# Seven-product units of a feed-forward layer: four weight sums in a row, and the offset tokens read from a copy in the first unit alone

## The chip, the core and the metric

One core of one Trainium2 chip runs the whole program. The metric is the device time of one execution in microseconds (us). TensorE (PE in the profile; its weight loads are PEld) multiplies, VectorE (DVE), ScalarE (ACT) and GpSimd (POOL) work on tiles in SBUF, and SyncE (SP) issues most transfers.

## The reference

A two-layer transformer over 256 latent and 256 context tokens, width 1024: in each layer a half feed-forward block, a mixer (attention, then mLSTM), and a second half feed-forward block. What the change touches is the first product of the feed-forward block:

```python
def half_ffn(h, shift, scale, gate, w_in, w_out, g, b):
    xm = modulate(h, shift, scale)
    a, u = jnp.split(xm @ w_in, 2, axis=-1)
    y = (jax.nn.silu(a) * u) @ w_out
    return post_norm(h, 0.5 * gate * y, g, b)
```

with D_FF = 2816, so `w_in` is 1024 x 5632, that is 22 blocks of 128 columns of `a` and as many of `u`.

## The kernel before

**Numbers.** Every fp32 operand of a product is held as a high part (fp32r) and a low part, the rest that the high part leaves out. `split` (L223 to L229) makes them: ACT casts to the high part (L224), DVE subtracts it to get the low part (L229). `mm3` (L238 to L245) does one product in three matmuls: high by high, high by low, low by high. All of them are recorded under L240. The split tokens are `xh` and `xl` (t3 and t4 in the order of instructions); 512 tokens are the columns, 256 latent (LAT) and 256 context (CTX).

**The units.** A feed-forward block runs over 22 units j, in two halves of 11 (`NFH`). A unit multiplies a column block of `w_in` with all tokens; after 11 units, `unit_out` multiplies the half's result with `w_out`. In the second half of two of the four blocks (second block of layer 0, first block of layer 1) the unit is `fast_in`: seven products of half size in place of eight (Strassen's scheme, in the form of Winograd). For this the tokens are combined once, ahead of the stage, in `fast_sums`, which runs beside the last `unit_out` products of the first half: it leaves one combination in the place of CTX tokens of `xh`/`xl` and puts three more, `made[0]`, `made[1]`, `made[2]`, into one tile (L582 to L587; t1185 in the first stage, t1681 in the second). The weights of a unit are combined anew in each unit: two raw chunks r0 and r1 (512 KB each) hold the blocks a11, a21, a12, a22, and four sums s1 to s4 are made of them by DVE (L625). Seven of these go through `split`: a11 alone, r1 (a12 and a22), s1 with s2, s4 with s3.

**The products of a unit,** in PE's order: a11, a12, s1, s2, a22, s4, s3. Each is 4 steps of 3 matmuls with 256 columns, 12 matmuls, so a unit has 84. Between them ACT copies results out of PSUM: L650 after a11 and L653 after s1 (both before the same PSUM tile is added to, by s2 and by s4), L655 after s2, L657 after a22. Then DVE adds (L659), ACT applies silu (L660), DVE forms the product (L663, L664), and the result is split for `unit_out`.

**Where the operands lie.** Split weights lie 16 elements (64 bytes) into their tile (`SH`). Six of the seven token operands begin on a multiple of 256 bytes. `made[2]`, the one of the product a22, begins `FLIP` = 56 elements (224 bytes) past one:

```python
x = self.t([P, 6 * n + FLIP], F32R, pool=st)
at = [2 * i * n + (FLIP if i == 2 else 0) for i in range(3)]
```

**Buffers and order.** Split weights live in a pool of 7 tiles (`WB`, tag "w"), which all stages share, raw chunks in a pool of 3 (`RAW`). The order of instructions on each engine is made by the framework's scheduler from the program's order and the pools; each engine runs its own row in order and waits at semaphores.

Of the kernel before, what the change touches and what calls it, by code (L numbers as in the profile page):

```python
# [9 lines left out]
F32 = mybir.dt.float32  # L10
F32R = mybir.dt.float32r
# [7 lines left out]
P = 128  # L19
# [3 lines left out]
TL = 256  # L23
# [4 lines left out]
NFH = 11  # L28
# [3 lines left out]
BLOCK = 64  # L32
# [11 lines left out]
WB = 7  # L44
# [45 lines left out]
FLIP = 56  # L90
# [81 lines left out]
class Body:  # L172
# [74 lines left out]
    def x(self, d, g):  # L247
        return self.xh[:, d, g[0] : g[1]], self.xl[:, d, g[0] : g[1]]
# [333 lines left out]
    def fast_operands(self, st):  # L582

        n = ND // 2 * TL
        x = self.t([P, 6 * n + FLIP], F32R, pool=st)
        at = [2 * i * n + (FLIP if i == 2 else 0) for i in range(3)]
        self.made = [[x[:, a + p * n : a + (p + 1) * n].rearrange("p (k f) -> p k f", f=TL) for p in range(2)] for a in at]  # L587

    def fast_sums(self, i):

# [25 lines left out]
    def fast_in(self, j, w_in, st):  # L616

        nc, V, S = self.nc, self.nc.vector, self.nc.scalar
        half = 4 * P
        r0, r1 = (self.raw(w_in[2 * j + i]) for i in range(2))  # L620
        sums = self.t([P, 4 * half], tag="sums", bufs=1, pool=st)
        part = lambda x, i: x[:, i * half : (i + 1) * half]
        a11, a21, a12, a22 = part(r0, 0), part(r0, 1), part(r1, 0), part(r1, 1)
        s1, s2, s4, s3 = (part(sums, i) for i in range(4))
        add = lambda o, x, y: V.tensor_tensor(out=o, in0=x, in1=y, op=ALU.add)  # L625
        ws = [self.pair(sh=SH, n=half)] + [self.pair(sh=SH) for _ in range(3)]
        self.split(a11, *ws[0])
        self.split(r1, *ws[1])
        add(s1, a21, a22)
        add(s2, s1, a11)  # L630
        self.split(sums[:, : 2 * half], *ws[2])
        add(s4, s2, a12)
        add(s3, a11, a21)
        self.split(sums[:, 2 * half :], *ws[3])
        w = {n: [part(x, i) for x in ws[p]] for n, p, i in (
            ("a11", 0, 0), ("a12", 1, 0), ("a22", 1, 1), ("s1", 2, 0), ("s2", 2, 1), ("s4", 3, 0), ("s3", 3, 1),
        )}
        of = lambda k0, g: lambda k: self.x(k0 + k, g)
        made = lambda i: lambda k: [x[:, k, :] for x in self.made[i]]

        def product(o, name, x, first, last):
            for k in range(ND // 2):
                c = slice(k * P, (k + 1) * P)
                self.mm3(o, [y[:, c] for y in w[name]], x(k), first and k == 0, last and k == ND // 2 - 1, group=False)

        x, yv, z = self.mm()[:, :TL], self.mm(), self.mm()[:, :TL]
        y, v = yv[:, :TL], yv[:, TL:]
        a, u = self.tmp(), self.tmp()
        product(x, "a11", of(0, LAT), True, False)
        S.copy(a[:, :TL], x)  # L650
        product(y, "a12", of(ND // 2, LAT), True, True)
        product(v, "s1", of(0, CTX), True, False)
        S.copy(u[:, TL:], v)  # L653
        product(x, "s2", made(0), False, False)
        S.copy(a[:, TL:], x)  # L655
        product(z, "a22", made(2), True, True)
        S.copy(u[:, :TL], z)  # L657
        product(v, "s4", of(ND // 2, CTX), False, True)
        V.tensor_tensor(out=a, in0=a, in1=yv, op=ALU.add)  # L659
        S.activation(a, a, AF.Silu)  # L660
        product(x, "s3", made(1), False, True)
        u2 = u.rearrange("p (n f) -> p n f", n=2)
        V.scalar_tensor_tensor(u2, x[:, None, :].broadcast_to([P, 2, TL]), -1.0, u2, ALU.mult, ALU.subtract)  # L663
        V.tensor_tensor(out=a, in0=a, in1=u, op=ALU.mult)  # L664
        gh, gl = self.gt[j] = tuple(self.t([P, self.gw], F32R, tag=k, bufs=self.gn, pool=self.gp) for k in ("gh", "gl"))
        self.split(a, gh, gl)
# [1071 lines left out]
```

## Time and profile before

| | us |
|---|---|
| median of 3 runs (lowest to highest) | 1640.27 (1639.47 to 1640.42) |
| the profiled execution, its whole time | 1640.61 |
| its span, first to last instruction | 1638.8 |
| first `fast_in` stage (11 units) | about 747 to 854 |
| second `fast_in` stage (11 units) | about 1102 to 1209 |

In the page, busy time is given for each engine with its share of the span; then groups of instructions by line, with their count, their busy time, the mean of one in ns, and the idle time of the engine just before them. In the timeline each row has the start, the time, the engine, the line and operation, tiles and sizes, a count, and in brackets the idle time before it with what ended it. A row of stretches has the stretch, its length, then for each engine the busy time and in brackets how many instructions ran, the granted PE clock as a share of full speed, and the share of the DMA engines with GB/s.

### The profile page before, as it was taken

What the parts mean: (1) busy time and instruction counts of PE and PEld (TensorE: products, weight loads), DVE (VectorE), ACT (ScalarE), POOL (GpSimd) and SP (SyncE); (2) the same over time, 40 slices, a digit from 0 to 9 for tenths busy, and PEclk for the clock granted to TensorE, in tenths of its full rate; (3) what the DMA queues carried; (4) which work ended last, traced back from release to release, by engine and by line L of the source; (5) the groups of instructions that cost most, each with busy time, mean ns of one, the idle gap of its engine ahead of it and who ended that gap; (6) DMA issues with size and microseconds to landing.
All of it is one profiled execution on the core that took longest, in us unless ns stands there. A gap on an engine that the chain in (4) does not pass through costs nothing. (4 is left out here: it accounts for less than half of the span.)

```text
span 1638.8 us, 26592 instructions
## 1 busy us (share of the span) xinstructions
PE 1616.8 (99%) x10308; PEld 1455.5 (89%) x10308; DVE 1353.5 (83%) x2689; ACT 745.4 (45%) x1269; POOL 62.0 (4%) x76
## 2 busy tenths in 40 slices
PE   9999999999999999999999999999999999999998
PEld 6888888889988998889998998889999989999987
DVE  5899977749889879899976979699966968897687
ACT  5622123214676443325652434335652657566542
POOL 0000000001011100000000100000001000020000
PEclk9999999999999999999999999999999999999999
DMA  9677766422202447633344258713363332437552
GB/s 362 221 232 245 238 198 193 140 78 85 65 2 78 150 134 220 218 115 117 116 145 177 78 161 289 252 63 110 103 220 102 97 129 91 139 102 251 181 176 92
DMA packets 72495, 252.59 MB, mean 154 GB/s; under 512 B 7984, under 2 KB 10800, under 8 KB 72368
## 3 DMA queue, kind: packets, MB, share of 16 engines
q1 hardware_dynamic: 71792, 250.10, 47.3%
q8 instruction: 81, 1.33, 0.3%
q10 hardware_dynamic: 576, 0.79, 0.1%
q14 instruction: 46, 0.38, 0.1%
HBM read 249.81 MB, written 1.05 MB: 153 GB/s over the span
## 5 line engine op out<-in xcount | busy, mean ns | idle before, releaser
L240 PE MATMUL t<-t,t 128*128 128x256 f32 (+2 forms) x8412 | 1323.0, 318 | 6.7 <-ACT t L224 3.1
L240 PEld LDWEIGHTS t<-t,t 128*128 128x128 f32 x8412 | 1191.7, 188 | 125.7 <-ACT t L224 4.6
L224 ACT CAST t<-t 128x1024 fp32r<-128x1024 f32 (+3 forms) x521 | 429.6, 844 | 493.8 <-PE t L240 232.8
L229 DVE TENSOR_TENSOR t<-t,t 128x256 fp32r<-128x256 f32 (+2 forms) x740 | 514.8, 729 | 119.1 <-ACT t L224 114.7
L340 DVE SCALAR_TENSOR_TENSOR t<-t,t 128x1024 bf16<-128x1024 f32 x224 | 260.7, 1219 | 0.0
L578 ACT ACTIVATE t<-t 128x512 f32<-128x512 f32 (+1 forms) x71 | 34.4, 489 | 107.4 <-PE t L240 107.4
L920 PE MATMUL t<-t,t 128*128 128x256 f32 (+1 forms) x256 | 79.3, 310 | 0.0
L922 PE MATMUL t<-t,t 128*128 128x256 f32 (+1 forms) x256 | 78.6, 307 | 0.0
L921 PE MATMUL t<-t,t 128*128 128x256 f32 (+1 forms) x256 | 78.3, 306 | 0.0
L702 DVE SCALAR_TENSOR_TENSOR t<-t,t,t 128x256 f32<-128x256 f32 x96 | 42.8, 478 | 41.4 <-PE t L240 41.2
L579 DVE TENSOR_TENSOR t<-t,t 128x512 f32<-128x512 f32 (+1 forms) x71 | 39.1, 553 | 44.5 <-PE t L240 30.8
L474 POOL TENSOR_TENSOR t<-t,t 128x256 f32<-128x256 f32 x30 | 23.3, 775 | 1117.2 <-ACT t L464 1115.7
L1435 PE MATMUL t<-t,t 128*128 128x512 f32 (+3 forms) x286 | 61.0, 368 | 1.7 <-ACT t L1512 1.0
L1435 PEld LDWEIGHTS t<-t,t 128*128 128x128 f32 (+2 forms) x286 | 43.8, 159 | 19.1 <-issue 3.7
L848 PE MATMUL t<-t,t 128*128 128x512 f32 (+1 forms) x300 | 60.5, 364 | 0.0
L848 PEld LDWEIGHTS t<-t,t 128*128 128x128 f32 x300 | 51.5, 189 | 9.0
L464 ACT ACTIVATE t<-t 128x256 f32<-128x256 f32 x72 | 26.1, 412 | 65.2 <-DVE t L457 65.2
L921 PEld LDWEIGHTS t<-t,t 128*128 128x128 f32 x256 | 48.1, 188 | 3.0 <-DVE t L229 0.5
L920 PEld LDWEIGHTS t<-t,t 128*128 128x128 f32 x256 | 48.2, 188 | 2.7
L922 PEld LDWEIGHTS t<-t,t 128*128 128x128 f32 x256 | 48.2, 188 | 2.6 <-DVE t L532 0.2
L625 DVE TENSOR_TENSOR t<-t,t 128x512 f32<-128x512 f32 x66 | 45.3, 687 | 1.2 <-DMA t<-in_ffn_in 0.6
L531 ACT ACTIVATE t<-t,t 128x256 fp32r<-128x256 f32 x72 | 32.8, 503 | 27.4 <-DVE t L530 27.4
(200 smaller groups left out, 1064.9 us busy)
## 6 DMA issues: line engine op xcount, KB each, us to landing
t<-in_ffn_in SPq DMA_DIRECT2D x168, 512.0 KB, 4.1
t<-in_ada_w SPq DMA_DIRECT2D x137, 512.0 KB, 4.3
t<-in_ffn_out SPq DMA_DIRECT2D x66, 512.0 KB, 4.4
t<-in_ffn_last SPq DMA_DIRECT2D x22, 512.0 KB, 3.6
t<-in_att_in SPq DMA_DIRECT2D x12, 512.0 KB, 3.5
t<-in_c SPq DMA_DIRECT2D x8, 512.0 KB, 7.1
t<-in_att_out SPq DMA_DIRECT2D x8, 512.0 KB, 3.5
t<-in_ml_qk SPq DMA_DIRECT2D x8, 512.0 KB, 3.8
```

Of the source, the lines that this page charges most:

```text
L224: self.behind(self.nc.scalar.copy(h, x))
L229: self.behind(self.nc.vector.tensor_tensor(out=ls, in0=xs, in1=hs.bitcast(F32), op=ALU.subtract))
L240: mm = lambda *k, **kw: self.nc.tensor.matmul(*k, skip_group_check=not group, **kw)
L340: ins = nc.vector.scalar_tensor_tensor(self.tmp().bitcast(BF16), r, 1.0, self.cb[:, v, :], ALU.mult, ALU.mult, accum_out=to)
L579: V.tensor_tensor(out=sl, in0=sl, in1=pu[:, :n], op=ALU.mult)
L625: add = lambda o, x, y: V.tensor_tensor(out=o, in0=x, in1=y, op=ALU.add)
L702: V.scalar_tensor_tensor(z, y[:, gg[0] - t0 : gg[1] - t0], gate()[:, v, d : d + 1], z, ALU.mult, ALU.add)
L848: pin(nc.tensor.matmul(o, gs[g], ws[k][w][:, i : i + n], start=k == k0 and g == w == 0, stop=k == k1 - 1 and g == 1,))
L920: mm(o, self.xh[:, k, c], wh, start=k == 0, stop=False)
L921: mm(o, self.xh[:, k, c], wl, start=False, stop=False)
L922: mm(o, self.xl[:, k, c], wh, start=False, stop=k == ND - 1)
L1435: mm = lambda *k, **kw: pin(nc.tensor.matmul(*k, **kw))
```

## The change

The sum and copy of the third token combination now stand like this. `made[2]` lies right behind the other two, on a multiple of 256 bytes; a spare tile of `FLIP` elements keeps the size of what the stage holds. In the first unit of each stage (j = 11) a tile of the weight pool is taken, ACT copies both halves of `made[2]` into it `FLIP` elements past its start, and the product a22 of this unit reads the copy; in the ten units behind it, a22 reads `made[2]` itself. In every unit the four sums are made in a row, and both splits of sums follow.

```diff
     def fast_operands(self, st):
         n = ND // 2 * TL
-        x = self.t([P, 6 * n + FLIP], F32R, pool=st)
-        at = [2 * i * n + (FLIP if i == 2 else 0) for i in range(3)]
-        self.made = [[x[:, a + p * n : a + (p + 1) * n].rearrange("p (k f) -> p k f", f=TL) for p in range(2)] for a in at]
+        x = self.t([P, 6 * n], F32R, pool=st)
+        self.t([P, FLIP], pool=st)
+        self.made = [[x[:, (2 * i + p) * n : (2 * i + p + 1) * n].rearrange("p (k f) -> p k f", f=TL) for p in range(2)] for i in range(3)]
...
     def fast_in(self, j, w_in, st):
         half = 4 * P
+        t4 = self.made[2]
+        if j == NFH:
+            w = self.t([P, 2 * 1024 + BLOCK], F32R, tag="w", bufs=WB)
+            t4 = [w[:, FLIP + i * 1024 : FLIP + (i + 1) * 1024].rearrange("p (k f) -> p k f", f=TL) for i in range(2)]
+            for i in range(2):
+                S.copy(t4[i], self.made[2][i].bitcast(F32))
...
         add(s1, a21, a22)
         add(s2, s1, a11)
-        self.split(sums[:, : 2 * half], *ws[2])
         add(s4, s2, a12)
         add(s3, a11, a21)
+        self.split(sums[:, : 2 * half], *ws[2])
         self.split(sums[:, 2 * half :], *ws[3])
...
-        product(z, "a22", made(2), True, True)
+        product(z, "a22", lambda k: [x[:, k, :] for x in t4], True, True)
```

The lines of the changed kernel are six further down from L620 on (L625 becomes L631, L650 becomes L656).

On PE, where the product a22 of the first unit of the first stage stands (t3 and t4 are `xh` and `xl`, t1185 holds the made sums; right of the arrow tokens, then weights), before:

```order
L240 MATMUL t1216_7168<-t4_68,t1213_7153 128x256
L240 MATMUL t1216_7168<-t3_67,t1213_7153 128x256
L240 MATMUL t1215_7167<-t1185_6936,t1213_7153 128x256 x12
L240 MATMUL t1217_7169<-t1185_6936,t1212_7152 128x256 x12
L240 MATMUL t1216_7168<-t3_67,t1214_7154 128x256
```

and now:

```order
L240 MATMUL t1218_7172<-t4_68,t1215_7157 128x256
L240 MATMUL t1218_7172<-t3_67,t1215_7157 128x256
L240 MATMUL t1217_7171<-t1185_6936,t1215_7157 128x256 x12
L240 MATMUL t1219_7173<-t1209_7147,t1214_7156 128x256 x12
L240 MATMUL t1218_7172<-t3_67,t1216_7158 128x256
```

The count and order of matmuls stay; the twelve of a22 read t1209, the copy, where they read t1185.

On ACT, from the splits of `fast_sums` to the first copy out of PSUM of the first unit, before (the casts of a11 and of r1, into t1211 and t1212, stand ahead of these rows, in front of those of `fast_sums`):

```order
L224 CAST t1185_6936<-t1199_7046 128x512
L224 CAST t1185_6936<-t1198_7044 128x512
L224 CAST t1185_6936<-t1201_7059 128x512
L224 CAST t1213_7153<-t1210_7150 128x1024
L224 CAST t1214_7154<-t1210_7150 128x1024
L224 CAST t1225_7273<-t1222_7268 128x512
L224 CAST t1226_7274<-t1223_7270 128x1024
L650 COPY t1218_7170<-t1215_7167 128x256
```

and now:

```order
L224 CAST t1185_6936<-t1200_7047 128x512
L224 CAST t1185_6936<-t1199_7045 128x512
L224 CAST t1185_6936<-t1202_7060 128x512
L625 CAST t1209_7147<-t1185_6936 128x1024
L224 CAST t1213_7155<-t1210_7150 128x512
L625 CAST t1209_7147<-t1185_6936 128x1024
L224 CAST t1214_7156<-t1211_7152 128x1024
L224 CAST t1215_7157<-t1212_7154 128x1024
L224 CAST t1216_7158<-t1212_7154 128x1024
L224 CAST t1227_7277<-t1224_7272 128x512
L224 CAST t1228_7278<-t1225_7274 128x1024
L656 COPY t1220_7174<-t1217_7171 128x256
```

The two copies (L625) are new, and the casts of a11 (t1213) and r1 (t1214) of the first unit now stand behind the last cast of `fast_sums`, one behind each copy.

On DVE, the work on the weights of the third unit of the first stage and on the output of its first unit, before:

```order
L625 TENSOR_TENSOR t1238_7394<-t1236_7390,t1237_7392 128x512
L229 TENSOR_TENSOR t1239_7395<-t1236_7390,t1239_7395 128x512
L625 TENSOR_TENSOR t1238_7394<-t1238_7394,t1236_7390 128x512
L625 TENSOR_TENSOR t1238_7394<-t1236_7390 128x512
L659 TENSOR_TENSOR t1218_7170<-t1218_7170,t1216_7168 128x512
L229 TENSOR_TENSOR t1240_7396<-t1237_7392,t1240_7396 128x1024
L663 SCALAR_TENSOR_TENSOR t1219_7171<-t1215_7167,t1219_7171 128x512
L229 TENSOR_TENSOR t1241_7397<-t1238_7394,t1241_7397 128x1024
L664 TENSOR_TENSOR t1218_7170<-t1218_7170,t1219_7171 128x512
L625 TENSOR_TENSOR t1238_7394<-t1238_7394,t1237_7392 128x512
L229 TENSOR_TENSOR t1221_7265<-t1218_7170,t1220_7264 128x512
L229 TENSOR_TENSOR t1242_7398<-t1238_7394,t1242_7398 128x1024
```

and now:

```order
L229 TENSOR_TENSOR t1241_7399<-t1238_7394,t1241_7399 128x512
L665 TENSOR_TENSOR t1220_7174<-t1220_7174,t1218_7172 128x512
L229 TENSOR_TENSOR t1242_7400<-t1239_7396,t1242_7400 128x1024
L669 SCALAR_TENSOR_TENSOR t1221_7175<-t1217_7171,t1221_7175 128x512
L631 TENSOR_TENSOR t1240_7398<-t1238_7394,t1239_7396 128x512
L670 TENSOR_TENSOR t1220_7174<-t1220_7174,t1221_7175 128x512
L631 TENSOR_TENSOR t1240_7398<-t1240_7398,t1238_7394 128x512
L631 TENSOR_TENSOR t1240_7398<-t1238_7394 128x512
L229 TENSOR_TENSOR t1223_7269<-t1220_7174,t1222_7268 128x512
L631 TENSOR_TENSOR t1240_7398<-t1240_7398,t1239_7396 128x512
L229 TENSOR_TENSOR t1243_7401<-t1240_7398,t1243_7401 128x1024
L229 TENSOR_TENSOR t1244_7402<-t1240_7398,t1244_7402 128x1024
```

The same twelve stand there in another order: the fourth sum (L631, from t1239) now comes ahead of the low part of the first pair (t1243), and the sums stand further back among the work of the unit before.

## The prediction, made before the changed kernel ran

> **What bounds the kernel now.** The page first. TensorE is busy for 99% of the span, nearly all of it in L240, and that line waited 6.7 us in all.
>
> ```profile
> span 1638.8 us, 26592 instructions
> ...
> PE 1616.8 (99%) x10308; PEld 1455.5 (89%) x10308; DVE 1353.5 (83%) x2689; ACT 745.4 (45%) x1269; POOL 62.0 (4%) x76
> ...
> L240 PE MATMUL t<-t,t 128*128 128x256 f32 (+2 forms) x8412 | 1323.0, 318 | 6.7 <-ACT t L224 3.1
> ```
>
> So time comes only from the spacing of matmuls or from a wait of PE. The stretches of two neighbouring units of the first seven-product stage, cut where their first products start, show no idle PE and the full granted clock (1.00), yet one is 9.7 us long and the other 9.8.
>
> ```profile
> 776.30:786.00 9.70, 9.70 (x87) 9.70 (x86) 9.61 (x14) 6.08 (x10) 0.00 (x0) 1.00 0.38 113
> 786.00:795.80 9.80, 9.80 (x87) 9.80 (x86) 8.98 (x13) 5.99 (x10) 0.00 (x0) 1.00 0.33 110
> ```
>
> Where inside a unit the difference arises is read from ACT's timeline: its copies out of PSUM wait for PE, so their starts mark the ends of products (L653 after s1, L655 after s2, L657 after a22). In the second stage:
>
> ```profile
> 1109.51 0.37 ACT L657 COPY t<-t 128x256 f32<-128x256 f32 x1 [0.52 <-PE t L240]
> ...
> 1116.33 0.37 ACT L653 COPY t<-t 128x256 f32<-128x256 f32 x1 [0.47 <-PE t L240]
> 1117.68 0.38 ACT L655 COPY t<-t 128x256 f32<-128x256 f32 x1 [0.99 <-PE t L240]
> ...
> 1119.09 0.37 ACT L657 COPY t<-t 128x256 f32<-128x256 f32 x1 [0.52 <-PE t L240]
> ...
> 1126.16 0.37 ACT L653 COPY t<-t 128x256 f32<-128x256 f32 x1 [0.67 <-PE t L240]
> 1127.57 0.37 ACT L655 COPY t<-t 128x256 f32<-128x256 f32 x1 [1.04 <-PE t L240]
> ...
> 1129.00 0.37 ACT L657 COPY t<-t 128x256 f32<-128x256 f32 x1 [0.54 <-PE t L240]
> ...
> 1138.58 0.37 ACT L657 COPY t<-t 128x256 f32<-128x256 f32 x1 [0.51 <-PE t L240]
> ```
>
> From the end of a22 to the end of the next unit's s1 lie five products (s4, s3, a11, a12, s1). They take 1116.33 - 1109.51 = 6.82 us the first time, 1.364 a product, and 1126.16 - 1119.09 = 7.07 the next, 1.414 a product. From a22 to a22 it is 9.58, 9.91, 9.58 us: PE has **two paces, and each a22 turns one into the other**. The groups of matmuls by shape, in five stretches, say the same (the number after the busy time is the mean of one in ns): 747.2 to 752.4 and 1102.5 to 1107.9 (first units), 757.0 to 762.2 (second unit), 936 to 960 and 1535 to 1563 (256-column work elsewhere).
>
> ```profile
> L240 PE MATMUL t<-t,t 128*128 128x256 f32 x46 | 5.6, 281 | 0.0
> L240 PE MATMUL t<-t,t 128*128 128x256 f32 x49 | 5.9, 281 | 0.0
> L240 PE MATMUL t<-t,t 128*128 128x256 f32 x48 | 5.6, 276 | 0.0
> L240 PE MATMUL t<-t,t 128*128 128x256 f32 x206 | 24.4, 281 | 0.0
> L240 PE MATMUL t<-t,t 128*128 128x256 f32 x250 | 28.5, 276 | 0.0
> ```
>
> A mean of 281 ns goes with the slow pace (24.28 us over 206 matmuls is 118 ns apart, 1.414 for twelve), 276 with the quick one (28.28 over 250 is 113 ns, 1.357 for twelve). Both first units begin slow. And both paces hold for 24 us and more where nothing disturbs them.
>
> **The change part by part.**
>
> *The offset tokens.* a22 is the only product whose tokens begin 224 bytes past a multiple of 256, and the only place where the pace turns in these stages. With the copy, the first unit's a22 still reads at that offset and turns slow into quick; the ten behind it read on a whole 256 bytes, as s2 and s3 do, which turn nothing. So I expect quick from the first a22 on. What it is worth, from the first and the last L657 of each stage:
>
> ```profile
> 754.28 0.37 ACT L657 COPY t<-t 128x256 f32<-128x256 f32 x1 [0.52 <-PE t L240]
> ...
> 851.71 0.37 ACT L657 COPY t<-t 128x256 f32<-128x256 f32 x1
> ```
>
> ```profile
> 1206.95 0.37 ACT L657 COPY t<-t 128x256 f32<-128x256 f32 x1
> ```
>
> Ten units, 70 products, take 851.71 - 754.28 = 97.43 us and 1206.95 - 1109.51 = 97.44. All quick they take 70 x 1.36 = 95.2 (1.36 lies between 1.357 and 1.364, the two readings of the quick pace). Gain: 2.23 + 2.24 = **4.5 us**; with 1.357 it is 4.9, with 1.364 it is 3.9. Before the first a22 nothing changes (slow), and behind the last one both kernels are quick, since eleven turns end like one. 512-column work has one pace in this trace, 214 in 48 us behind quick 256-column work (690) as behind slow (1050), so the gain isn't handed back there:
>
> ```profile
> 690.00:738.00 48.00, 48.00 (x214) 39.75 (x213) 47.97 (x86) 11.11 (x15) 0.00 (x0) 1.00 0.38 121
> 1050.00:1098.00 48.00, 48.00 (x214) 39.74 (x213) 39.46 (x68) 12.31 (x16) 0.00 (x0) 1.00 0.35 114
> ```
>
> *Two copies on ACT per stage, and the casts that now stand behind them.* The copies are of 128 x 1024, like the casts of that size below (1.05 us), so 4.2 us in all on an engine that is 45% busy. What counts is whether the first unit's weights come in time. ACT, then DVE, ahead of the first stage:
>
> ```profile
> 739.33 0.62 ACT L224 CAST t<-t 128x512 fp32r<-128x512 f32 x1 [2.32 <-DVE t L613]
> 742.00 1.05 ACT L224 CAST t<-t 128x1024 fp32r<-128x1024 f32 x1 [2.05 <-DVE t L625]
> 743.20 1.57 ACT L224 CAST t<-t 128x1024 fp32r<-128x1024 f32 x2 [0.15 <-DVE t L625]
> 746.13 1.05 ACT L224 CAST t<-t 128x1024 fp32r<-128x1024 f32 x1 [1.35 <-DMA t<-in_ffn_in]
> ```
>
> ```profile
> 740.22 0.67 DVE L229 TENSOR_TENSOR t<-t,t 128x512 fp32r<-128x512 f32 x1
> ...
> 743.08 3.03 DVE L229 TENSOR_TENSOR t<-t,t 128x1024 fp32r<-128x1024 f32 x3
> ```
>
> The last cast of the token sums ends at 739.95. Behind it, in the new order: high copy to 741.0, a11 to 741.6, low copy (its source is done at 740.9) to 742.7, r1 to 743.7, the two sum casts to 744.8 and 745.8. DVE's low parts (1.2 us each for 1024) follow: r1 at 744.9, s1 and s2 at 746.1, s4 and s3 at 747.3. PE begins the stage at about 747.0 (five slow products, 7.07, ahead of 754.28, less some 0.2 us from the last matmul to the copy) and needs a12 at 748.4, s1 at 749.8, s4 at 754.1. The least margin is 3.5 us. In the second stage the same casts have two more us:
>
> ```profile
> 1092.28 0.62 ACT L224 CAST t<-t 128x512 fp32r<-128x512 f32 x1 [3.71 <-DVE t L613]
> ```
>
> ends at 1092.90, against a start at 1109.51 - 7.27 = 1102.2, so 9.3 us where the first stage has 7.0. I take 0; if this cover were gone, the price is the copies' own time, up to 2.1 us a stage. Below nothing it can't be: PE has no wait here that it could lose.
>
> *The order of the sums, and a faster PE.* DVE does the same work. Can it keep up with 9.52 us a unit? Two L659 in a row, one unit apart, and the waits of the first stage (total, times, longest):
>
> ```profile
> 776.76 0.68 DVE L659 TENSOR_TENSOR t<-t,t 128x512 f32<-128x512 f32 x1
> ...
> 785.84 0.68 DVE L659 TENSOR_TENSOR t<-t,t 128x512 f32<-128x512 f32 x1
> ```
>
> ```profile
> DVE t L229 <- ACT t L224: 8.0, 10, 2.2
> ```
>
> 785.84 - 776.76 = 9.08 us without a wait, and it idled 0.8 us a unit. So 0.44 us a unit stays free, and the sums' new place costs 0 while it does. The tightest meeting is s4, which adds to the tile that ACT's L653 must have read. In the second unit of the first stage:
>
> ```profile
> 762.22 0.36 ACT L653 COPY t<-t 128x256 f32<-128x256 f32 x1
> ...
> 763.86 0.37 ACT L657 COPY t<-t 128x256 f32<-128x256 f32 x1 [0.48 <-PE t L240]
> ```
>
> The copy ends at 762.58, s4 starts at about 763.6: 1.0 us, since two casts stood ahead of it. The quick pace takes at most 9.81 - 9.52 = 0.3 of that in the next unit, and DVE wins it back. The sums in a row let the pair of s4 be split sooner and that of s1 up to 1.2 us (two sums) later. The cover for this is the lead of the weights: here the pair of s1 of the fifth unit, whose cast waits for PE to free a buffer,
>
> ```profile
> 776.50 1.05 ACT L224 CAST t<-t 128x1024 fp32r<-128x1024 f32 x1 [1.41 <-PE t L240]
> ```
>
> is cast in the fourth, 12 us ahead of its product (786.0 plus two products, 788.8), and DVE needs 1.2 of that. So I take 0; without the cover it is at most 1.2 us a unit.
>
> *Transfers.* No DMA is added. r0 is free once its last sum is made, and that sum now comes ahead of the splits, so the next chunk isn't asked for later.
>
> **Sum.** 1640.61 (the profiled execution, span 1638.8 and 1.8 around it) - 4.5 = 1636.1. The median of the runs shown is 1640.27, 0.34 below that execution, so I predict **1635.8 us**.
>
> **The rivals.**
>
> (1) *The offset isn't what turns the pace*: the place of a22 among ACT's and DVE's work is, and it goes on turning in each unit. Then the time stays at 1640.3. For it: the trace shows no addresses, and 930.29 below shows that a wait can turn the pace too. Against it: PE doesn't wait in a unit, and s2 and s3, which have such work beside them as well, never turn it.
> The Trainium skill (TensorE: Matmul & The Clock Gate, section "Back-to-back issue gap") gives the gap between matmuls from the columns alone, warm N/2.4 + 2.5 ns, an estimate of 109 ns for 256, with no term for where operands lie; by it moving them does nothing and this rival holds. The trace disagrees: 113 and 118 ns for the same columns at the same clock.
>
> (2) *The copy doesn't turn it* in one stage or in both, because another address decides and not the 224 bytes. Then all 70 products are slow, 70 x 1.414 = 99.0, a loss of 1.55 us, and 0.1 for the last two products. One stage failing gives 1640.3 - 2.24 + 1.65 = 1639.7, both 1643.6. Against it: 22 units, with weights in changing buffers, turned 22 times.
>
> (3) *A wait that nothing repairs* (slower). Before, a unit that fell slow was turned back by the next a22. Now nothing turns it. If L659 (the old L653) comes over 1.0 us later in the second unit, s4 waits, and PE may leave the wait in the other pace; here it did, from 281 to 276 (931.6 to 934.6 us), and can as well the other way:
>
> ```profile
> 930.29 1.05 PE L437 MATMUL t<-t,t 128*128 128x1 f32 x8 [0.58 <-DVE t L474]
> ```
>
> ```profile
> L240 PE MATMUL t<-t,t 128*128 128x256 f32 x29 | 3.5, 276 | 0.0
> ```
>
> Price: 65 products left x 0.054 = 3.5, plus 1.0 of wait, less 2.24: +2.3 a stage, 1644.8. For it: the 1.0 us margin and a different order on ACT. Against it: the margins above.
>
> **How the numbers follow.** Forecast 75%, no turn from the offset 4%, one stage failing 8%, both 4%, the wait 9%. The forecast's own range is 1634.3 to 1637.3: 0.5 either way from the quick pace, and about 1 us for 256-column work elsewhere, whose waits may come out in another pace after the shift. To leave out no more than two in ten, the range reaches up over one stage failing and no change: 1634.0 to 1640.4. About 0.2% (3.3 us) is what a measurement tells from no change: faster is below 1637.0, slower above 1643.5. Faster 0.73 (the forecast less its upper tail), same 0.15 (that tail, no turn, one stage), slower 0.12 (the wait, most of both failing).
>
> **What would show it.** Right: L663 (the old L657) every 9.52 us from the first unit on, 95.2 us over ten; means of 281 ns only up to the first a22 of a stage, 276 behind it; no wait of PE in either stage; the 512-column stages 2.2 and then 4.5 us earlier. Wrong: steps of 9.58 and 9.91 (rival 1), 9.90 throughout (rival 2), or a PE gap at s4 with 281 behind it (rival 3).

## The result, and the profile after

The changed kernel took 1633.54 us (median of 7 runs, 1632.96 to 1636.21), beside 1639.47 for the kernel before in 7 runs: a ratio of 0.9969, 95% interval 0.9959 to 0.9979. It was measured a second time, against 24 runs of the kernel before: 1634.82 (11 runs, 1633.17 to 1638.33), ratio 0.9976, interval 0.9967 to 0.9985. The forecast of 1635.8 against 1640.27 is a ratio of 0.9973 and lies inside both.

The page of the changed kernel's profiled execution (1633.42 us) has the same shape as before:

```profile
span 1631.6 us, 26590 instructions
...
PE 1610.0 (99%) x10308; PEld 1448.8 (89%) x10308; DVE 1350.8 (83%) x2689; ACT 748.9 (46%) x1273; POOL 62.0 (4%) x76
...
L240 PE MATMUL t<-t,t 128*128 128x256 f32 (+2 forms) x8412 | 1316.5, 317 | 6.4 <-ACT t L224 3.3
```

The count of matmuls is the same. PE's busy time fell by 6.8 us, of which 6.5 stand on L240, and its idle time there by 0.3 us. So hardly any of it was a wait; the same matmuls stand closer together. ACT has four instructions more, the two copies of each stage.

Where they stand closer is read, as before, from ACT's copies out of PSUM behind a22. This is ACT's timeline of the changed kernel, with L663 (L657 before) alone, in the first stage and then in the second:

```profile
753.41 0.37 ACT L663 COPY t<-t 128x256 f32<-128x256 f32 x1
...
762.95 0.37 ACT L663 COPY t<-t 128x256 f32<-128x256 f32 x1
...
772.47 0.38 ACT L663 COPY t<-t 128x256 f32<-128x256 f32 x1 [0.47 <-PE t L240]
...
848.63 0.37 ACT L663 COPY t<-t 128x256 f32<-128x256 f32 x1
...
1106.44 0.37 ACT L663 COPY t<-t 128x256 f32<-128x256 f32 x1
...
1115.98 0.37 ACT L663 COPY t<-t 128x256 f32<-128x256 f32 x1
1125.50 0.37 ACT L663 COPY t<-t 128x256 f32<-128x256 f32 x1 [0.47 <-PE t L240]
...
1201.66 0.37 ACT L663 COPY t<-t 128x256 f32<-128x256 f32 x1
```

Ten units take 848.63 - 753.41 = 95.22 us and 1201.66 - 1106.44 = 95.22, where they took 97.43 and 97.44. The alternation of 9.58 and 9.91 is gone: each step is 9.52 (9.54 for the first of each stage, since the s4 behind that a22 still takes 1.377 us; the products after it take 1.360). The groups of matmuls by shape, in five stretches of the changed kernel, name the pace: the first unit of the first stage up to its a22 (746.5 to 751.5), the second unit and more (756 to 768), units further on (780 to 840), then the same for the second stage (1099.5 to 1104, 1120 to 1200).

```profile
L240 PE MATMUL t<-t,t 128*128 128x256 f32 x45 | 5.5, 281 | 0.0
L240 PE MATMUL t<-t,t 128*128 128x256 f32 x108 | 12.4, 276 | 0.0
L240 PE MATMUL t<-t,t 128*128 128x256 f32 x532 | 60.5, 276 | 0.0
L240 PE MATMUL t<-t,t 128*128 128x256 f32 x40 | 4.9, 281 | 0.0
L240 PE MATMUL t<-t,t 128*128 128x256 f32 x709 | 80.5, 276 | 0.0
```

281 ns, the slow pace, stands ahead of the first a22 only; behind it 276 holds to the end of the stage. From the start of a stage's first matmul to the start of the first matmul behind the stage, by the trace's own times, both stages now take 105.0 us, where they took 107.23: twice 2.23, so **4.47 us** in all. A product of 12 matmuls, read in the same way, takes 1.413 us in the slow pace and 1.360 in the quick one.

The two profiles differ by more than that, 7.2 us of span. Laid side by side matmul by matmul, 0.56 us lie in the first 26 us of the program and some 1.8 us between 1430 and 1525 us; the rest are pieces of 0.2 to 0.5 us of either sign. The groups of 256-column matmuls from 1450 to 1525 us, of the kernel before and then of the changed one, are of work that the change doesn't touch:

```profile
L240 PE MATMUL t<-t,t 128*128 128x256 f32 x516 | 63.3, 283 | 0.8 <-DVE t L532 0.5 <-DVE t L229 0.2
```

```profile
L240 PE MATMUL t<-t,t 128*128 128x256 f32 x575 | 69.2, 280 | 0.6 <-DVE t L532 0.6
```

The waits there are alike, the mean is 283 in one and 280 in the other. The second profile of the changed kernel, the same program, has a span of 1635.0 us, 3.3 us above the first, with both stages at 105.0 again. So a difference of this size outside the stages comes between two executions of one kernel too, and is no effect of the change.

### The profile page after: what moved, and what is told of

Read it like the earlier page. It is cut to its first block, busy times and chain, and to the rows that moved or that the text cites. A ratio compares the mean times of both kernels' runs of the same rounds, so it can differ in the third digit from the quotient of the medians.

```text
span 1631.6 us, 26590 instructions
## 1 busy us (share of the span) xinstructions
PE 1610.0 (99%) x10308; PEld 1448.8 (89%) x10308; DVE 1350.8 (83%) x2689; ACT 748.9 (46%) x1273; POOL 62.0 (4%) x76
## 3 DMA queue, kind: packets, MB, share of 16 engines
HBM read 249.81 MB, written 1.05 MB: 154 GB/s over the span
## 5 line engine op out<-in xcount | busy, mean ns | idle before, releaser
L240 PE MATMUL t<-t,t 128*128 128x256 f32 (+2 forms) x8412 | 1316.5, 317 | 6.4 <-ACT t L224 3.3
L240 PEld LDWEIGHTS t<-t,t 128*128 128x128 f32 x8412 | 1185.2, 188 | 125.6 <-ACT t L224 5.0
L631 DVE TENSOR_TENSOR t<-t,t 128x512 f32<-128x512 f32 x66 | 45.3, 687 | 0.4
```

The lines of the kernel that those rows point to most:

```text
L240: mm = lambda *k, **kw: self.nc.tensor.matmul(*k, skip_group_check=not group, **kw)
```

## The experiments

Where the length of a stage, a product or a stretch is given without a row, it is the difference of start times of matmuls in the trace. A kernel with one time and no bounds was executed once; what is read from it is the pace in its trace, not its time. Where operands lie is taken from the programs: with the addresses of the built ones, all tokens of the two stages other than those moved here begin on a multiple of 256 bytes, and all weights 64 bytes past one.

**Each part of the change alone.** First the changed kernel without its copy, so that every a22 reads on a whole 256 bytes:

```diff
-        if j == NFH:
-            w = self.t([P, 2 * 1024 + BLOCK], F32R, tag="w", bufs=WB)
...
-                S.copy(t4[i], self.made[2][i].bitcast(F32))
```

> The changed kernel without its copy: a22 reads made[2] on a whole 256 bytes in all 22 units, nothing is read 224 bytes past. If the offset alone turns the pace: both stages enter slow and stay slow, 77 products x 1.414 = 108.9 us a stage (before 107.2, changed 105.0), 3.3 us slower than the kernel before, means of 281 ns throughout. If the place of a22 in the unit turns it (rival 1): steps of 9.58 and 9.91 us go on, 107.2 a stage. If aligned tokens are quick by themselves: 77 x 1.36 = 104.7.

It took 1642.80 us (1641.61 to 1645.67), ratio to before 1.0025, interval 1.0015 to 1.0036: slower than before, and some 8 us slower than the changed kernel. ACT's timeline, the copy behind a22 (L658 in this kernel), and the matmuls from 748 to 850 us:

```profile
754.35 0.37 ACT L658 COPY t<-t 128x256 f32<-128x256 f32 x1 [0.52 <-PE t L240]
764.25 0.37 ACT L658 COPY t<-t 128x256 f32<-128x256 f32 x1 [0.52 <-PE t L240]
...
853.29 0.37 ACT L658 COPY t<-t 128x256 f32<-128x256 f32 x1
```

```profile
L240 PE MATMUL t<-t,t 128*128 128x256 f32 x868 | 102.4, 281 | 0.0
```

98.94 us over ten units, 9.89 each: with nothing at the offset, the pace with which the stage began stays to its end. That is the state that the second rival named (1643.6 if the copy failed in both stages).

Then the order of the sums alone, on the kernel before:

```diff
-        self.split(sums[:, : 2 * half], *ws[2])
         add(s4, s2, a12)
         add(s3, a11, a21)
+        self.split(sums[:, : 2 * half], *ws[2])
```

> The kernel before with only the four sums in a row ahead of both splits. If this part is worth nothing, as I took it: stages of 107.2 us each, the pace turning in every a22, the time that of the kernel before within its scatter. If the order of the sums is a part of the gain beyond the 4.5 us of the pace: faster than before by 1 to 2 us, with the loss of time found outside the two stages.

1639.19 us, ratio 1.0003, interval 0.9994 to 1.0012. Both stages took 107.23 us as before, and a22 (L657) turns the pace each time:

```profile
753.59 0.37 ACT L657 COPY t<-t 128x256 f32<-128x256 f32 x1 [0.52 <-PE t L240]
...
763.17 0.37 ACT L657 COPY t<-t 128x256 f32<-128x256 f32 x1 [0.52 <-PE t L240]
...
773.08 0.37 ACT L657 COPY t<-t 128x256 f32<-128x256 f32 x1 [0.54 <-PE t L240]
...
851.02 0.37 ACT L657 COPY t<-t 128x256 f32<-128x256 f32 x1
```

9.58, 9.91, and 97.43 over ten. So the order of DVE's work neither costs nor brings anything, and it isn't what turns the pace. This kernel's profile also had 1.8 us less than that of before from 1430 to 1525 us (93.25 beside 95.07), as the changed kernel's had (93.25). The order, which both share, isn't the cause: the second profile of the changed kernel took 94.31 there, and the kernel before with its a22 at 96 and 192 bytes (below), which has the old order, 93.23. So this part is scatter.

The changed kernel itself, once more beside these:

> The changed kernel once more. The two stages again 105.0 us each in the profile. Measured gain so far 5.9 us by medians, 5.2 by means, of which the stages explain 4.5. If the rest is the pace of 256-column work elsewhere, as waits happen to leave it: the gain comes nearer to 4.5 with more runs, and the stretches outside the stages differ from the first profile of the changed kernel by up to 2 us. If the rest belongs to the change: 5 to 6 us again, and the same stretches short again.

1634.82 us and 0.9976, as told above; its stages took 105.0 us each.

**Is it the offset, or is it the copy?** The same copy, put at 0 bytes past a multiple of 256 in the first stage and at 32 in the second (the numbers in the code count elements of 4 bytes):

```diff
+OFFS = (0, 8)
...
-            t4 = [w[:, FLIP + i * 1024 : FLIP + (i + 1) * 1024].rearrange("p (k f) -> p k f", f=TL) for i in range(2)]
+            self.stage = getattr(self, "stage", -1) + 1
+            o = OFFS[self.stage]
+            t4 = [w[:, o + i * 1024 : o + (i + 1) * 1024].rearrange("p (k f) -> p k f", f=TL) for i in range(2)]
```

> The changed kernel with the copy of the first unit placed 0 bytes past a multiple of 256 in the first stage and 32 bytes past one in the second. If the offset turns the pace and not the copying: the first stage stays slow, 108.9 us. If the copying or its place on ACT does it: 105.0. Second stage: if any start off a multiple of 64 bytes turns the pace, 105.0; if 224 bytes is needed, 108.9.

1642.82 us. Both stages stay slow, 108.83 and 108.84 us; the groups of matmuls from 748 to 850 and from 1106 to 1210 us:

```profile
L241 PE MATMUL t<-t,t 128*128 128x256 f32 x869 | 102.5, 281 | 0.0
L241 PE MATMUL t<-t,t 128*128 128x256 f32 x885 | 104.4, 281 | 0.0
```

With the copy at 0, everything that the change added is there (the tile, ACT's work, the moved casts) and the gain is not. The offset makes it. 32 bytes don't turn the slow pace: a22 alone took 1.421 us instead of 1.413, and behind it all was as before.

**How much of a22 must lie at the offset?** The copy at 224 bytes again, but read by the first two of a22's four steps in the first stage (6 matmuls), and by the first step in the second (3 matmuls):

```diff
+STEPS = (2, 1)
...
-        t4 = self.made[2]
+        t4, off = self.made[2], 0
         if j == NFH:
+            self.stage = getattr(self, "stage", -1) + 1
+            off = STEPS[self.stage]
...
-        product(z, "a22", lambda k: [x[:, k, :] for x in t4], True, True)
+        product(z, "a22", lambda k: [x[:, k, :] for x in (t4 if k < off else self.made[2])], True, True)
```

> The changed kernel, but only the first two of the four steps of the first a22 read the copy in the first stage (6 matmuls 224 bytes past), one of four in the second (3 matmuls); the others read made[2]. If the turn is made by a few matmuls at the offset: both stages 105.0 us. If it builds up over the product, as the spacing in the first s4 suggests (it settles only there): 108.8, the pace slow throughout, in the second stage at least.

1637.69 us: the first stage took 104.98 us, the second 108.83. The groups from 760 to 850 and from 1112 to 1205 us:

```profile
L241 PE MATMUL t<-t,t 128*128 128x256 f32 x797 | 90.5, 276 | 0.0
L241 PE MATMUL t<-t,t 128*128 128x256 f32 x792 | 93.4, 281 | 0.0
```

Six matmuls turn the pace, three don't. The two counts were tried in different stages; where both stages read the same offset, in all other runs, they behaved alike.

**Which offsets turn it, and which way?** On the kernel before, `made[2]` moved from 224 bytes to 64 in the first stage and 128 in the second, then to 96 and 192 (`(24, 48)` in place of `(16, 32)`), for all eleven a22 of a stage:

```diff
-        at = [2 * i * n + (FLIP if i == 2 else 0) for i in range(3)]
+        self.stage = getattr(self, "stage", -1) + 1
+        at = [2 * i * n + ((16, 32)[self.stage] if i == 2 else 0) for i in range(3)]
```

> The kernel before with made[2] 64 bytes past a multiple of 256 in the first stage and 128 in the second, read there by a22 in all 22 units. 224 bytes turned the pace each time, 0 and 32 did not. If the place within 256 bytes decides: one of the two may turn each unit as 224 did (107.2 us a stage). If only starts off a multiple of 64 bytes can turn it: both stages slow throughout, 108.8 us.

> The same with 96 bytes in the first stage and 192 in the second. If starts off a multiple of 64 turn it when they are far enough from 0 and 32: 96 turns (107.2 us), 192 does not (108.8). If nearness to the next multiple of 256 decides: 192 turns, or neither.

64 and 128 took 1639.62 us, with stages of 105.83 and 108.83; the groups from 760 to 850 and from 1106 to 1210 us:

```profile
L240 PE MATMUL t<-t,t 128*128 128x256 f32 x789 | 90.4, 277 | 0.0
L240 PE MATMUL t<-t,t 128*128 128x256 f32 x882 | 104.0, 281 | 0.0
```

128 bytes never turn the slow pace. 64 bytes turn it in the first unit, and then every a22 leaves the quick pace behind it: 9.60 us a unit, in which a22 takes 1.421 and s4 behind it 1.379. That was a miss: no outcome that I had named has a stage that turns once and then stays quick.

96 and 192 took 1635.39 us, with stages of 105.59 and 105.97. That was a miss as well: I had expected 96 to turn both ways like 224, and 192 to turn nothing. The copy behind a22 (L658) in the first stage:

```profile
754.30 0.37 ACT L658 COPY t<-t 128x256 f32<-128x256 f32 x1 [0.51 <-PE t L240]
763.87 0.37 ACT L658 COPY t<-t 128x256 f32<-128x256 f32 x1 [0.51 <-PE t L240]
773.45 0.37 ACT L658 COPY t<-t 128x256 f32<-128x256 f32 x1 [0.51 <-PE t L240]
...
850.09 0.38 ACT L658 COPY t<-t 128x256 f32<-128x256 f32 x1
```

Every step is 9.58 (the first 9.57), with no 9.91 between: 96 bytes, and 192 as well, turn slow to quick and leave quick quick. What is lost against 9.52 lies in a22 itself (1.403 at 96, 1.428 at 192) and in s4 behind it (1.377 and 1.385).

From the quick pace 32 and 128 bytes were still open. In the changed kernel, with the first unit's copy at 224 as it is, the later a22 were put there:

```diff
-        x = self.t([P, 6 * n], F32R, pool=st)
-        self.t([P, FLIP], pool=st)
...
+        x = self.t([P, 6 * n + FLIP], F32R, pool=st)
+        self.stage = getattr(self, "stage", -1) + 1
+        at = [2 * i * n + ((8, 32)[self.stage] if i == 2 else 0) for i in range(3)]
...
```

> The changed kernel with its later a22 (units 1 to 10) reading at 32 bytes past a multiple of 256 in the first stage and at 128 in the second; the first unit still turns the pace by its copy at 224. It shows what these two offsets do to the quick pace; from the slow one neither turned it. If an offset that doesn't turn slow doesn't turn quick either (my theory: 0, 32 and 128 turn nothing, 64, 96 and 192 turn to quick, 224 turns both ways): units of 9.52 us, 105.0 a stage, or some 0.03 more a unit where a22 itself is slower at that offset. Rival, such an offset turns quick to slow: 9.9 us a unit from unit 2 on, about 108.4 a stage.

1638.39 us, with stages of 108.58 and 105.60. The theory held for 128 and fell for 32. The copy behind a22 (L664) in the first stage, then the matmuls of the second from 1115 to 1205 us:

```profile
754.31 0.37 ACT L664 COPY t<-t 128x256 f32<-128x256 f32 x1
...
763.90 0.37 ACT L664 COPY t<-t 128x256 f32<-128x256 f32 x1
...
773.80 0.37 ACT L664 COPY t<-t 128x256 f32<-128x256 f32 x1 [0.53 <-PE t L240]
...
853.00 0.37 ACT L664 COPY t<-t 128x256 f32<-128x256 f32 x1
```

```profile
L240 PE MATMUL t<-t,t 128*128 128x256 f32 x792 | 90.5, 277 | 0.0
```

One unit is quick (9.59), then the a22 at 32 bytes leaves the slow pace, and ten a22 at 32 bytes never bring it back: 9.90 a unit to the end. At 128 bytes a22 takes 1.414 us, as long as in the slow pace, yet the product behind it is quick again (1.366, then 1.360).

**Can more be had?** Two steps were tried together: a22 first in the first unit, so that four more products are quick (0.2 us a stage), and in the three 256-column tails of feed-forward blocks copies of four tiles at 224 bytes, to turn these too.

```diff
+        def third():
+            product(z, "a22", lambda k: [x[:, k, :] for x in t4], True, True)
+            S.copy(u[:, :TL], z)
+
+        if j == NFH:
+            third()
...
-        product(z, "a22", lambda k: [x[:, k, :] for x in t4], True, True)
-        S.copy(u[:, :TL], z)
+        if j > NFH:
+            third()
...
+                    if hf and d == ND - TAIL and g == LAT and i < 4:
+                        gs = turn[i]
...
```

> The changed kernel, with a22 first in the first unit of each stage (four products fewer at the slow pace, 0.2 us a stage), and the same trick at the three places where unit_out goes over from 512 to 256 columns (around 346, 882 and 1235 us): ACT copies the latent half of four result tiles 224 bytes past a multiple of 256 into a tile of the weight pool, and the first unit there reads them. If reads at that offset turn the pace in any 256-column work: 276 ns behind the first 12 matmuls there until the first wait of PE, some 15 us x 3.7% = 0.6 us at each place, in all 1 to 3 us faster than the changed kernel. If the turn belongs to the seven products: only the 0.4 us. If the taken tile makes the next weights late: slower than the changed kernel.

It failed: 1641.58 us, ratio 1.0017, interval 1.0008 to 1.0026. Both stages were slow throughout, 108.8 us each, although the copies of the tails did what was hoped (the numbers stand below, with the last run). Which step did it was told apart by the first alone:

> The changed kernel with a22 of the first unit ahead of a11 (its copy at 224 is the first thing that PE reads in the stage), nothing else. In the run that had this and the copies for the three tails together, both stages were slow throughout (1.413 us a product). Theory: the place of a22 did that, since behind 512-column work the pace isn't yet settled when the offset is met, and 224 bytes turn whatever they find; then both stages are slow here too, about 108.8 us each, and the time is some 7 to 8 us above the changed kernel's. Rival, the tails' copies did it: both stages quick, 104.8 us (four more products at 1.36 than the changed kernel's).

1643.03 us, both stages slow (11 units of 9.893 us, 108.8); the groups from 746 to 850 and from 1104 to 1210 us:

```profile
L240 PE MATMUL t<-t,t 128*128 128x256 f32 x878 | 103.6, 281 | 0.0
L240 PE MATMUL t<-t,t 128*128 128x256 f32 x902 | 106.4, 281 | 0.0
```

So the place of a22 did it in the stages. Where its twelve matmuls come right behind 512-column work, the product behind them is slow; four slow products later in the same unit, they leave the quick pace. But the 512-column work alone doesn't explain it: the copies for the tails in the run before, also at 224 bytes and right behind 512-column work, left the quick pace in all three tails. There, by the programs, the weights of the twelve matmuls lie on a multiple of 256 bytes, and those of a22 64 past one. Whether that is the difference wasn't tried.

Last, the changed kernel with its stages as they are, and the tails' copies at 96 bytes, which in the stages left the quick pace whatever they found:

```diff
...
+                    w4 = self.t([P, 2 * 1024 + BLOCK], F32R, tag="w", bufs=WB)
+                    turn = [[w4[:, 24 + p * 1024 + i * TL :][:, :TL] for p in range(2)] for i in range(4)]
+                    for i in range(4):
+                        for p in range(2):
+                            nc.scalar.copy(turn[i][p], self.gt[hf * NFH + i][p][:, :TL].bitcast(F32))
```

> The changed kernel with nothing moved in the stages, and in each of the three 256-column tails of feed-forward blocks the first four steps (12 matmuls) of the first latent product reading copies of gt at 96 bytes past a multiple of 256, which turned slow to quick and left quick alone in the stages. A tail has 264 matmuls of 256 columns; slow to quick is 4.5 ns each, so at most 1.2 us a tail, 3.6 in all. Theory: stages 105.0 us each as in the changed kernel, means of 276 to 279 ns in the tails where the changed kernel has 283, and 1 to 3.5 us less than the changed kernel: ratio to before 0.995 to 0.997. Rival, waits and other products inside the tails set the pace anew: means stay at 282 or 283 and the time is that of the changed kernel, ratio 0.997 to 0.998; the eight copies on ACT may then cost up to 1 us.

1633.84 us (1631.74 to 1634.54, 5 runs), ratio to before 0.9966, interval 0.9952 to 0.9979: as fast as the changed kernel, and not to be told from it. The tails gained in parts. The matmuls of 880 to 900 us, the second tail, of the changed kernel and then of this one:

```profile
L240 PE MATMUL t<-t,t 128*128 128x256 f32 x153 | 18.6, 283 | 0.0
```

```profile
L240 PE MATMUL t<-t,t 128*128 128x256 f32 x153 | 18.1, 279 | 0.0
```

0.5 us there; in the windows of the other two tails the mean falls less (283 to 281 from 340 to 375 us, 283 to 282 from 1230 to 1280). The starts of the matmuls say why. The first 108 matmuls of a tail take 12.74 us in every tail of the eleven profiles without copies there, 12.34 with these copies at 96 bytes and 12.31 with those at 224: behind the copies the pace is quick in all three tails. Then two matmuls of another line (L437) come in between, and behind them either pace can follow, whichever was there before. Twelve matmuls behind them take 1.360 us in the first two tails of this kernel and 1.413 in the third; in the second tail of the changed kernel they take 1.413 in its first profile and 1.360 in its second. So the theory held up to L437 and the rival behind it: the copies are worth 0.4 us a tail, 1.2 in all, which these runs can't tell from nothing, and the pace behind L437 differs between two executions of one program.

## Why the prediction was right

**The two paces and what turns them: right, and shown.** After, the changed kernel's units are 9.52 us from the first a22 on, no later a22 turns anything, and 281 ns stands ahead of the first one only. The run without the copy and the run with the copy at 0 bytes show that the offset of the tokens is the cause. The first rival (the place of a22 among other work turns the pace) falls with these two, in which a22 keeps its place and nothing turns, and with the order-only run, which moved that work and kept the turns.

How the same stretches of 90 us read in the view of stretches (the numbers in brackets count the instructions of PE, PEld, DVE, ACT and POOL; behind them the granted clock), in the changed kernel and then in the one without the copy:

```profile
760.00:850.00 90.00, 90.00 (x796) 90.00 (x795) 83.83 (x110) 58.97 (x97) 0.00 (x0) 1.00 0.41 129
1110.00:1200.00 90.00, 90.00 (x797) 90.00 (x796) 85.60 (x113) 57.84 (x95) 0.00 (x0) 1.00 0.39 121
```

```profile
760.00:850.00 90.00, 90.00 (x766) 90.00 (x766) 81.93 (x107) 55.71 (x92) 0.00 (x0) 1.00 0.37 113
1110.00:1200.00 90.00, 90.00 (x767) 90.00 (x766) 80.01 (x105) 55.28 (x92) 0.00 (x0) 1.00 0.35 106
```

PE is busy for all of both, at the full clock, and does 30 matmuls more in one than in the other. By the Trainium skill (TensorE: Matmul & The Clock Gate, section "Back-to-back issue gap") the isolated gap follows from the columns and the clock alone, which makes an estimate of 109 ns for 256 columns. For a stream of weight loads and matmuls the same section says that both set the spacing, and it has no term for where the tokens lie. The runs show such a stream with two spacings, 113 and 117.5 ns (90 us over 796 and 766), and which of the two holds is decided by one a22 of eleven.

**The size: right to the hundredth in the stages, with some luck.** 2.23 + 2.24 was worked out from 70 products at 1.36; measured 2.23 and 2.23, with 69 of the 70 at 1.360 and the first s4 at 1.377. 1.36 had been taken between two readings that give 4.9 and 3.9 us, and neither reading is the pace alone: 1.357 spreads 28.28 us over 250 matmuls, whose starts span 28.22 us in 249 steps (113.3 ns, 1.360 for twelve), and 1.364 has in it the s4 behind a22, at 1.377. The price of the second rival can be checked as well: it gave 1643.6 for both stages slow, and the kernel without the copy, which is that case, took 1642.80; by the stages alone it lost 1.59 us each against 1.55 + 0.1 expected.

**ACT's copies at nothing: right.** ACT's timeline of the changed kernel ahead of the first stage (L625 are the copies; the start of the stage is 746.15), then L659 of the second unit and of the third:

```profile
737.92 0.63 ACT L224 CAST t<-t 128x512 fp32r<-128x512 f32 x1 [1.79 <-DVE t L613]
738.59 1.06 ACT L625 CAST t<-t 128x1024 fp32r<-128x1024 f32 x1
739.54 0.62 ACT L224 CAST t<-t 128x512 fp32r<-128x512 f32 x1
740.06 1.05 ACT L625 CAST t<-t 128x1024 fp32r<-128x1024 f32 x1
741.01 3.46 ACT L224 CAST t<-t 128x1024 fp32r<-128x1024 f32 x4
...
760.31 0.36 ACT L659 COPY t<-t 128x256 f32<-128x256 f32 x1
...
770.66 0.36 ACT L659 COPY t<-t 128x256 f32<-128x256 f32 x1
```

The copies take 1.06 and 1.05 us, and the last row, four casts, ends at 744.47, 1.7 us ahead of the stage, in the order that was worked out.

**The order of the sums at nothing, and DVE's lead: right.** The order-only run gives 1.0003. The margin at s4, the third rival's place, grew in the second unit: L659 ends at 760.67, and s4 starts five products after the unit's start of 755.95, at 762.75. That is 2.1 us, where it was 1.0. Two casts stand ahead of the copy as before, but they begin at 758.75, 2.8 us into the unit, where they began 3.9 us into it (760.66). The tightest unit is now the third, which the prediction didn't look at: its L659 ends at 771.02 and its s4 starts at 772.27, 9.52 us behind that of the second, which leaves 1.2 us. No wait of PE stands in either stage; the list of waits of the changed kernel from 746.2 to 851 us begins

```profile
ACT t L224 <- PE t L240: 13.1, 9, 1.9
ACT t L661 <- PE t L240: 8.1, 9, 1.0
DVE t L229 <- ACT t L224: 5.2, 6, 2.1
```

and has no row in which PE waits.

**The total: inside the range as a ratio, below it in microseconds.** 1633.54 stands against 1635.8 and lies 0.5 us under the range's lower end of 1634.0. The kernel before came out lower too, 1639.47 beside the 1640.27 from which the forecast was made; against its own base the changed kernel has 0.9969, and the range from 1634.0 to 1640.4 is 0.9962 to 1.0001 of 1640.27. The second measurement, 1634.82 beside 1639.07, gives 4.25 us by the medians, where the first gave 5.93 and the stages alone give 4.47. So the mechanism's 4.47 us are what the change brings, and what the first measurement has beyond them is the term "about 1 us for 256-column work elsewhere", which was sized too small: two profiles of the changed kernel differ by 3.3 us of span with the stages alike, and its 18 runs reach from 1632.96 to 1638.33. Over all thirteen profiles the work that lies at 400 to 560 us in that of before, ahead of both stages, differs in length by 2.0 us. A part of such differences is set behind the matmuls of L437, as the tails show; what sets the rest was not traced further.

## What to carry to other kernels

Where PE is busy throughout, it can still lose time in the spacing of its matmuls: take groups of one shape in several stretches of the trace, and where their means differ at the same clock (281 and 276 ns here), look for the place where one turns into the other, from the copies that mark the ends of products. If an operand that lies off the multiple of 256 bytes marks that place, a copy of that operand read once can bring a whole stage into the quick pace; here six matmuls behind four products of the same shape were enough, and 64, 96 or 192 bytes past a multiple of 256 were safer than 224, since they never turned quick into slow. And a change that moves the pace on purpose needs a look at all its units in the trace, because neither a wait nor a busy share shows it.

## What the runs showed of the hardware

In these stages matmuls of 256 columns have two paces, 113.3 and 117.8 ns apart (1.360 and 1.413 us for twelve), and keep the one they are in while all tokens lie on a multiple of 256 bytes: the slow one for 108.8 us (the run without the copy), the quick one for the 98 us behind the first a22 (the changed kernel). Behind other 256-column work, the offset of the tokens of twelve matmuls decides what follows them:

| bytes past a multiple of 256 | from the slow pace | from the quick pace |
|---|---|---|
| 0 | stays slow | stays quick |
| 32 | stays slow | turns slow |
| 64, 96, 192 | turns quick | stays quick, a22 itself 1.40 to 1.43 us |
| 128 | stays slow | stays quick, a22 itself 1.414 us |
| 224 | turns quick | turns slow |

At 224 bytes each a22 turned the pace, 22 times in the profile of before; at 32 the turn from quick to slow was seen once, since the pace never came back. I had expected one rule for all offsets that turn, and it takes at least three kinds. What in the chip makes the two paces, whether the offset counts by itself or against that of the weights (64 bytes in both stages of all runs), and why twelve matmuls at 224 bytes right behind 512-column work leave the slow pace in the stages and the quick one in the tails, stays open.
